# Both group norms of a hybrid attention/LRU layer: root and reciprocal on all partitions, in place of a column that is spread afterwards

## The chip, the cores and the metric

The kernel runs on one core of one Trainium2 chip. The metric is the device time of one execution in microseconds (us). The engines are named as in the profile: PE is TensorE (PEld its weight loads), ACT is ScalarE, DVE is VectorE, POOL is GpSimd, and SP is the engine whose queue issues most of the DMAs.

## The reference

One layer of an encoder: a norm, one input projection, attention on one half of the channels, a gated linear recurrence (LRU) on the other half, a norm of each half, a gate, and the output projection. Sequence 512, model width 2048, all in float32.

```python
def rms_norm(x, w):
    xf = x.astype(jnp.float32)
    y = xf * lax.rsqrt(jnp.mean(xf * xf, axis=-1, keepdims=True) + EPS)
    return (y * w.astype(jnp.float32)).astype(x.dtype)

def hybrid_layer(x, norm_w, w_in, ...):
    h = rms_norm(x, norm_w)
    proj = jnp.einsum('bsd,de->bse', h, w_in)
    q, k, v, g_attn, xr, g_lru = jnp.split(proj, SPLITS, axis=-1)
    attn_out = attention_group(q, k, v, q_norm_w, k_norm_w)      # 1024 channels
    lru_out = lru_group(xr, conv_w, conv_b, ...)                  # 1024 channels
    mixed = jnp.concatenate([rms_norm(attn_out, attn_norm_w) * jax.nn.silu(g_attn),
                             rms_norm(lru_out, lru_norm_w) * jax.nn.silu(g_lru)], axis=-1)
    return x + jnp.einsum('bse,ed->bsd', mixed, w_out)
```

The change concerns the two `rms_norm` calls on `attn_out` and `lru_out`: for each of the 512 tokens, one number, 1/sqrt(mean of 1024 squares + EPS).

## The kernel before

**Layout.** Both groups' outputs lie with channels on the 128 partitions and tokens along the free axis (128x512 tiles), so the sum of squares of one token runs over partitions as well as over tiles. Tiles are first squared and added (on ACT, DVE and POOL) into one 128x512 tile: `sums["l"]` (named `hsum` in the trace) for the LRU group, `sums["a"]` (`asum`) for the attention group. What is left is a sum over the 128 partitions for each of 512 tokens, the root and the reciprocal, and the result laid on all partitions as `gbc` (128x512), since every channel of a token is multiplied by it (`normed`).

**How the norm is made.** `group_rstd` multiplies four 128x128 blocks of the sums, as stationary operands, by a column of ones (`L817`), which puts tokens on partitions: a 128x4 tile `r_l` or `r_a`. DVE copies it from PSUM, POOL does the mean and the power -0.5 (`rsqrt_mean`, L343 and L344). `rows` then splits the four columns into a high and a low part, writes each into a diagonal (`ident` times the column, L357), and multiplies a matrix of ones by both (L364), so that the 512 numbers stand on all partitions; DVE copies that into `gbc` (L365).

**The float32 scheme.** Each product of two float32 matrices is three products of their high and low parts (`mm3`, L153 to L155). Of each weight tile `wr` that a DMA brings, ACT writes the high part `wh` (L218) and DVE the low part `wl` (L219); PE reads both. Work on PE is thus a steady stream of 128x512 products, each of which needs such a pair.

**What sets the order.** PE's instructions stand in the order in which the program writes them (generators `weave` fill work into a chain by counted steps, the numbers that `yield` returns). On ACT, DVE and POOL a scheduler chooses the order when the kernel is built; what stands in `tc.high_priority` goes ahead. On the chip each engine runs its instructions strictly in that order, and one that waits holds up all behind it.

**PSUM.** There are eight banks: four of kind `pj` for the projections and four of kind `mm`. A projection keeps four `pj` banks for its four token blocks or column blocks; the next projection writes the same four, so each must have been read out ("evacuated") before. For the query projections ACT does that (`ev<-pj`, L593); for the gate projections DVE does (L468).

**Where the two norms stand.** The LRU group's norm is in `kv`: `lru_squares` ends with an addition on POOL (L567), and the norm is made while the second query projection runs (its banks are those of the first query projection). The attention group's norm is in `later`, beside the last gate projection; its sum ends with an addition on POOL (L750) after the last attention head.

Of the kernel before, what the change touches and what calls it, by code (L numbers as in the profile page):

```python
# [12 lines left out]
F32R = mybir.dt.float32r  # L13
AF = mybir.ActivationFunctionType
# [3 lines left out]
P = 128  # L18
SEQ = 512
DM = 2048  # L20
KT = DM // P
NT = SEQ // P
HD = 128
NH = 8
NKV = 2
G = NH // NKV
NB = 8
EPS = 1e-6
# [35 lines left out]
def hybrid_kernel(  # L64
# [20 lines left out]
    nc = tc.nc  # L85
# [4 lines left out]
    pools, order = {}, {"left": [], "right": []}  # L90

    def opened(name, side):
        pools[name] = tc.alloc_tile_pool(name=name, bufs=1, side=side, reuse_waits="tile")
        order[side].append(name)
        return pools[name]
# [22 lines left out]
    def nm(s):  # L118
        cnt[0] += 1
        return f"{s}_{cnt[0]}"  # L120
# [22 lines left out]
    def mm():  # L143
        return ps.tile([P, SEQ], F32, tag="mm", name=nm("mm"))

    def const(shape, name, dt=F32):
        return cp.tile(list(shape), dt, tag=name, name=name)

    def f(ap):
        return ap.bitcast(F32)  # L150
# [9 lines left out]
    ones = const([P, P], "ones")  # L160
    nc.gpsimd.memset(ones, 1.0)
    ones_r = const([P, P], "ones_r", F32R)
# [178 lines left out]
    def rsqrt_mean(dst, src, n, width):  # L341

        nc.gpsimd.tensor_scalar(dst, src, 1.0 / n, EPS, op0=ALU.mult, op1=ALU.add)  # L343
        last_pool[0] = nc.gpsimd.tensor_tensor(dst, dst, nhalf[:, :width], op=ALU.pow).ins  # L344
# [4 lines left out]
    def rows(dst, col, dg):  # L349

        shape = [P, NT, P]
        part = [const([P, NT], nm("part")) for _ in range(2)]
        parts = [dg() for _ in part]
        nc.vector.tensor_copy(part[0].bitcast(F32R), col)
        nc.vector.tensor_sub(part[1], col, part[0])
        for c, d in zip(part, parts):
            nc.vector.tensor_mul(  # L357
                d, ident[:, None, :].broadcast_to(shape), c[:, :, None].broadcast_to(shape)
            )
        yield  # L360
        pb = mm()
        for k, d in enumerate(parts):
            d = d.rearrange("p t q -> p (t q)")
            nc.tensor.matmul(pb, ones_r, d, start=k == 0, stop=k == 1)  # L364
        nc.vector.tensor_copy(dst, pb)  # L365
        yield
# [59 lines left out]
    def drain(fill):  # L426
        for _ in fill:
            pass
# [30 lines left out]
    sums = {}  # L459
# [97 lines left out]
    def lru_squares():  # L557

        hsum = pools["rot"].tile([P, 2, SEQ], F32, tag="hsum", name="hsum")
        nc.scalar.activation(hsum, hp[0], AF.Square)  # L560
        for pair in hp[1:]:
            yield 2
            sq = pools["rot"].tile([P, 2, SEQ], F32, tag="hsq", bufs=1, name=nm("hsq"))
            nc.scalar.activation(sq, pair, AF.Square)
            nc.vector.tensor_add(hsum, hsum, sq)
        sums["l"] = hsum[:, 0, :]
        nc.gpsimd.tensor_add(sums["l"], sums["l"], hsum[:, 1, :])  # L567
# [29 lines left out]
    def norm_rope(es, nh, tab):  # L597

        es = [e[:, : nh * HD].rearrange("p (h d) -> p h d", d=HD) for e in es]
        rs = []  # L600
        for e in es:
            r = pools["rot"].tile([P, nh], F32, tag=f"rr{nh}", bufs=NT, name=nm("rr"))
            for h in range(nh):
                sq = pools["rot"].tile([P, HD], F32, tag="sh", bufs=1, name=nm("sh"))
                nc.scalar.activation(sq, e[:, h, :], AF.Square, accum_out=r[:, h : h + 1])
            rsqrt_mean(r, r, HD, nh)
            rs.append(r)
        for t, (e, r) in enumerate(zip(es, rs)):
            sq = pools["rot"].tile([P, nh, HD], F32, tag="sq", bufs=2, name=nm("sq"))
            nc.vector.tensor_mul(e, e, r[:, :, None].broadcast_to([P, nh, HD]))  # L610
            for s in range(2):
                nc.vector.tensor_mul(
                    sq.rearrange("p h (a s d) -> p h a s d", s=2, d=32)[:, :, :, s, :],
                    e.rearrange("p h (a s d) -> p h a s d", s=2, d=32)[:, :, :, 1 - s, :],
                    tab[:, t, 1, :].rearrange("p (a s d) -> p a s d", s=2, d=32)[:, None, :, s, :]
                    .broadcast_to([P, nh, 2, 32]),
                )
            nc.vector.tensor_mul(e, e, tab[:, t, 0, :][:, None, :].broadcast_to([P, nh, HD]))
            nc.vector.tensor_add(e, e, sq)
        return es  # L620
# [7 lines left out]
    def sent(es, nh, *us):  # L628

        us = us or [  # L630
            pools["rot"].tile([P, NQ, 2, NT, B], F32, tag="uq", bufs=2, name=nm("uq"))
            for _ in range(nh // 2)
        ]
        for n, u in enumerate(us):
            for t, e in enumerate(es):
                blocks(u, t, e[:, 2 * n : 2 * n + 2].rearrange("p h d -> p (h d)"))
            yield
            asides.append(put_aside(u, "qd", 5))

    def landed(aside_):  # L640

        to = pools["qkv"].tile([P, NQ, 2, NT, B], F32, tag="lq", bufs=2, name=nm("lq"))
        bring_back(to, aside_)
        return to

    def split_head(pair, k, hi, lo):
        src = pair[:, :, k]
        hi, lo = (in_order(v) for v in (hi, lo))
        nc.scalar.copy(hi, src)
        nc.vector.tensor_sub(lo, src, f(hi))  # L650

    def kv(es):
        turned_k = sent(norm_rope(es, NKV, rk), NKV)
        yield 20
        opened("wx", "right")
        for t in range(NT):
            vv = es[t][:, NKV * HD :]
            vt = aside(
                lambda *a: pools["qkv"].tile(*a, tag="v", bufs=NT, name=nm("v")), 2 * NKV * HD // H
            )  # L660
            vh[t], vl[t] = vt[:, 0, :], vt[:, 1, :]
            nc.scalar.copy(vh[t], vv)
            nc.vector.tensor_sub(vl[t], vv, f(vh[t]))
        yield from lru_squares()
        yield 2
        drain(turned_k)
        yield 6
        pair = landed(asides.pop(0))
        for h in range(NKV):
            yield (12, 4)[h]  # L670
            kt = pools["qkv"].tile([P, 2, SEQ], F32R, tag="kt", bufs=NKV, name=nm("kt"))
            kth[h], ktl[h] = kt[:, 0, :], kt[:, 1, :]
            split_head(pair, h, kth[h], ktl[h])
        r = group_rstd(sums["l"], "r_l", NB * P)
        yield 4
        drain(rows(
            gbc, r,
            lambda: pools["rope"].tile([P, NT, P], F32R, tag="kv", bufs=NT, name=nm("kv")),
        ))

    qs = {}

# [127 lines left out]
    def fin_s(shape=(P, SEQ), dt=F32):  # L810
        return pools["fin"].tile(list(shape), dt, tag="s", bufs=2, name=nm("s"))

    def group_rstd(src, name, n):

        pr = mm()
        for t in range(NT):
            nc.tensor.matmul(  # L817
                pr[:, t : t + 1], src[:, t * P : (t + 1) * P], ones[:, 0:1], start=True, stop=True
            )
        r = const([P, NT], name)  # L820
        nc.vector.tensor_copy(r, pr[:, :NT])
        rsqrt_mean(r, r, n, NT)
        return r

    gbc = const([P, SEQ], "gbc")

    def normed(pair):
        nc.vector.tensor_mul(pair, pair, gbc[:, None, :].broadcast_to([P, 2, SEQ]))
# [22 lines left out]
    def aside(tile_of, n):  # L851

        t = tile_of([P, n * H + 16], F32R)
        return t[:, 8 : 8 + n * H].rearrange("p (n e) -> p n e", e=H)
# [403 lines left out]

    fill = with_sums(both(), 3)
    weave(fill, kv(kvs))  # L1260
    drain(fill)

# [67 lines left out]
    def build(i, pair, parts):  # L1330
        mixed[i][1] = parts
        seven(pair, *parts)
# [4 lines left out]


    def later():
        yield 2  # L1340
        with tc.high_priority():
            r = group_rstd(sums["a"], "r_a", NH * HD)
        yield 4
        with tc.high_priority():
            drain(rows(gbc, r, lambda: fin_s((P, NT, P), F32R)))
        for pair in ap_[:2]:
            normed(pair)
        yield 4
        todo = gate(late, ap_[:2], R_AN, fin_s)
        for _ in range(3):  # L1350
            yield next(todo)
        build(4, ap_[0], [hring.tile([P, 7, H], F32R, name=nm(t)) for t in ("mh", "ml")])
        yield from todo
        for pair in ap_[2:]:
            normed(pair)

    acc = []
    wsums = last_sums()
    fill = with_sums(proj_feat(C_GA + SEQ, acc, take=take), 1, 8, 8 + 2 * NP)
    weave(fill, later())  # L1360
    drain(fill)
    closed("xw")
# [71 lines left out]
```

## Time and profile before

| | |
|---|---|
| median of 3 runs | 632.08 us (631.41 to 632.18) |
| the profiled execution | 632.23 us, of which the span is 630.1 us |
| PE | 623.8 us busy, 99% of the span, 2771 instructions |
| DVE | 491.4 us, 78%, 796 instructions |
| ACT | 348.2 us, 55%, 612 instructions |
| POOL | 104.4 us, 17%, 137 instructions |

Times in the profile are counted from the start of the span. A row of the timeline reads: start, duration, engine, line, operation, output<-input, shapes, count of merged instructions, and in square brackets the idle time of the engine before it with what ended it. Instructions on one engine overlap by some 0.08 us, so what an instruction adds on a busy engine is the distance between starts, not its duration.

### The profile page before, as it was taken

The numbers are of one execution on the slowest core, as the hardware profiler recorded it, in microseconds if no ns is written. First come the engines' busy times: TensorE is split into PE (matmuls) and PEld (weight loads), VectorE is DVE, ScalarE is ACT, GpSimd is POOL, SyncE is SP. The second block draws the span as 40 slices with busy tenths as digits, with TensorE's granted clock in tenths as the row PEclk, the third lists the DMA queues.
The fourth block names the chain that finished last, engine by engine and source line by source line (L and its number), as shares of the span: only waits on it lengthen the run. The fifth ranks groups of instructions, "written<-read, shape, count | busy, mean of one in ns | idle before, by whom it ended". The sixth has DMA issues, their size and how long they took to land.

```text
span 630.1 us, 8302 instructions
## 1 busy us (share of the span) xinstructions
PE 623.8 (99%) x2771; PEld 514.1 (82%) x2771; DVE 491.4 (78%) x796; ACT 348.2 (55%) x612; POOL 104.4 (17%) x137
## 2 busy tenths in 40 slices
PE   9999999999999999999999999999999999999997
PEld 6888888888888888888888888888888888888885
DVE  5967979986699874887887888549978866886885
ACT  3764899479945812545475447435445534443441
POOL 0000210112003632622123222100300001010010
PEclk9999999999999999999999999999999999999999
DMA  8977786859774599479668646924995677896162
GB/s 288 305 206 227 182 195 166 184 134 193 238 232 136 169 247 236 97 206 273 183 177 252 201 141 191 262 76 127 236 242 185 212 249 243 285 323 235 68 200 100
DMA packets 73594, 127.61 MB, mean 203 GB/s; under 512 B 6616, under 2 KB 29264, under 8 KB 73552
## 3 DMA queue, kind: packets, MB, share of 16 engines
q1 hardware_dynamic: 65664, 109.65, 55.8%
q0 software_dynamic: 7712, 17.31, 14.2%
q8 instruction: 21, 0.34, 0.2%
q14 instruction: 21, 0.17, 0.1%
q10 hardware_dynamic: 176, 0.14, 0.1%
HBM read 110.29 MB, written 37.75 MB: 235 GB/s over the span
## 4 chain that ended last, share of the span: by engine, by line
PE 96%; DMA 2%; SPq 1%; DVE 1%; issue 0%; DVEq 0%
PE pj L153 20%; PE pj L155 20%; PE pj L154 20%; PE mm L1023 14%; PE pj L1023 10%; PE mm L155 3%; PE mm L153 3%; PE mm L154 3%; DMA b<-in_x_dram 2%; SPq L206 0%; SPq L240 0%; PE mm L817 0%; DVE xu L281 0%; PE mm L364 0%; DVE b L272 0%
## 5 line engine op out<-in xcount | busy, mean ns | idle before, releaser
L154 PE MATMUL pj<-x,wh 128*128 128x512 f32 x376 | 146.6, 390 | 0.3 <-DVE x L261 0.3
L153 PE MATMUL pj<-x,wh 128*128 128x512 f32 x376 | 146.9, 391 | 0.0
L155 PE MATMUL pj<-x,wl 128*128 128x512 f32 x376 | 146.5, 390 | 0.2 <-DVE wl L219 0.2
L218 ACT CAST wh<-wr 128x512 fp32r<-128x512 f32 x143 | 85.7, 617 | 95.0 <-PE pj L154 37.0
L219 DVE TENSOR_TENSOR wl<-wr,wh 128x512 fp32r<-128x512 f32 x144 | 100.1, 723 | 20.0 <-ACT wh L218 19.2
L875 ACT CAST wh<-wr 128x1024 fp32r<-128x1024 f32 (+1 forms) x72 | 60.7, 860 | 75.0 <-PE mm L1023 37.5
L876 DVE TENSOR_TENSOR wl<-wr,wh 128x1024 fp32r<-128x1024 f32 (+1 forms) x72 | 68.7, 985 | 29.6 <-ACT wh L875 29.5
L155 PEld LDWEIGHTS pj<-x,wl 128*128 128x128 f32 x376 | 70.6, 188 | 15.4 <-DVE wl L219 0.6
L154 PEld LDWEIGHTS pj<-x,wh 128*128 128x128 f32 x376 | 70.6, 188 | 15.2 <-DVE x L261 0.7
L153 PEld LDWEIGHTS pj<-x,wh 128*128 128x128 f32 x376 | 70.6, 188 | 14.9
L153 PE MATMUL pj<-wh,x 128*128 128x512 f32 x192 | 74.8, 390 | 0.0
L155 PE MATMUL pj<-wh,x 128*128 128x512 f32 x192 | 74.7, 389 | 0.0
L154 PE MATMUL pj<-wl,x 128*128 128x512 f32 x192 | 74.7, 389 | 0.0
L899 POOL DMA_DIRECT2D t<-in_w_out_dram x40 | 33.7, 916 | 142.8 <-DMA t<-in_w_out_dram 99.3
L1023 PE MATMUL mm<-wh,ml 128*128 128x512 f32 x128 | 49.8, 389 | 0.0
L1023 PE MATMUL mm<-wh,mh 128*128 128x512 f32 x128 | 49.8, 389 | 0.0
L1023 PE MATMUL mm<-wl,mh 128*128 128x512 f32 x128 | 49.8, 389 | 0.0
L155 PEld LDWEIGHTS pj<-wh,x 128*128 128x128 f32 x192 | 36.0, 188 | 7.5
L153 PEld LDWEIGHTS pj<-wh,x 128*128 128x128 f32 x192 | 36.1, 188 | 7.5
L154 PEld LDWEIGHTS pj<-wl,x 128*128 128x128 f32 x192 | 36.1, 188 | 7.4
L705 POOL TENSOR_SCALAR p<-p,sm 128x512 f32<-128x512 f32 x32 | 24.2, 761 | 90.1 <-DVE sm L704 90.1
L1023 PE MATMUL pj<-wh,mh 128*128 128x512 f32 x96 | 37.4, 389 | 0.0
(209 smaller groups left out, 1035.2 us busy)
## 6 DMA issues: line engine op xcount, KB each, us to landing
wr<-in_w_in_dram SPq DMA_DIRECT2D x71, 512.0 KB, 5.0
wr<-in_w_out_dram SPq DMA_DIRECT2D x24, 512.0 KB, 5.3
t<-in_w_out_dram POOLq DMA_DIRECT2D x40, 256.0 KB, 7.5
wr<-t SPq DMA_DIRECT2D x40, 256.0 KB, 5.6
pd<-u SPq DMA_DIRECT2D x16, 512.0 KB, 3.0
pt<-pd SPq DMA_DIRECT2D x64, 128.0 KB, 4.0
t<-in_w_out_dram SPq DMA_DIRECT2D x24, 256.0 KB, 5.5
t<-t SPq DMA_DIRECT2D x16, 256.0 KB, 5.4
```

The costliest lines, as they stand in the source:

```text
L153: nc.tensor.matmul(acc, lh, rh, start=start, stop=False)
L154: nc.tensor.matmul(acc, lh, rl, start=False, stop=False)
L155: nc.tensor.matmul(acc, ll, rh, start=False, stop=stop)
L218: copy(hi, raw[:, k, :]).ins,
L219: nc.vector.tensor_sub(lo, raw[:, k, :], f(hi)).ins,
L705: last_pool[0] = nc.gpsimd.tensor_scalar(p, p, sm, 0.0, op0=ALU.mult, op1=ALU.add).ins
L875: nc.scalar.copy(hi[:, to], b)
L876: nc.vector.tensor_sub(lo[:, to], b, f(hi[:, to]))
L899: nc.gpsimd.dma_start(dst, src, accum_op=ALU.add)
L1023: nc.tensor.matmul(dst[s], lh[:, ts_], rh, start=i == 0 and j == 0, stop=i == 7 and j == 2)
```

## The change

`group_rstd` is gone, and the two norms don't use `rows` any more (it remains for the first norm, `rbc`). In their place stand `halved` and `spread`. `halved` splits the 128x512 sum into a high part (a copy on ACT) and a low part (a subtraction on DVE). `spread` multiplies the matrix of ones by both parts (two products, 128x512), which sums over the partitions and leaves each token's sum on all of them; ACT takes the root of sum/n + EPS from PSUM into `gbc` (it needs `eps`, a new 128x1 tile that POOL sets at the start), and DVE takes the reciprocal of `gbc` in place, 128x512. Nothing of it is left to POOL.

In `kv` the products stay where those of `rows` stood; in `later` they move six steps ahead, to where the four small products stood, and `halved` ahead of that.

```diff
@@ kv
-        r = group_rstd(sums["l"], "r_l", NB * P)
+        parts = halved(
+            sums["l"],
+            lambda: pools["rope"].tile([P, SEQ], F32R, tag="kv", bufs=NT, name=nm("kv")),
+        )
         yield 4
-        drain(rows(
-            gbc, r,
-            lambda: pools["rope"].tile([P, NT, P], F32R, tag="kv", bufs=NT, name=nm("kv")),
-        ))
+        spread(gbc, parts, NB * P)
@@
-    def group_rstd(src, name, n):
-
-        pr = mm()
-        for t in range(NT):
-            nc.tensor.matmul(
-                pr[:, t : t + 1], src[:, t * P : (t + 1) * P], ones[:, 0:1], start=True, stop=True
-            )
-        r = const([P, NT], name)
-        nc.vector.tensor_copy(r, pr[:, :NT])
-        rsqrt_mean(r, r, n, NT)
-        return r
+    eps = const([P, 1], "eps")
+    nc.gpsimd.memset(eps, EPS)
+
+    def halved(src, tile_of):
+
+        hi, lo = tile_of(), tile_of()
+        nc.scalar.copy(hi, src)
+        nc.vector.tensor_sub(lo, src, f(hi))
+        return hi, lo
+
+    def spread(dst, parts, n):
+
+        pb = mm()
+        for k, part in enumerate(parts):
+            nc.tensor.matmul(pb, ones_r, part, start=k == 0, stop=k == 1)
+        nc.scalar.activation(dst, pb, AF.Sqrt, scale=1.0 / n, bias=eps)
+        nc.vector.reciprocal(dst, dst)
@@ later
+        with tc.high_priority():
+            parts = halved(sums["a"], lambda: fin_s(dt=F32R))
         yield 2
         with tc.high_priority():
-            r = group_rstd(sums["a"], "r_a", NH * HD)
+            spread(gbc, parts, NH * HD)
         yield 4
-        with tc.high_priority():
-            drain(rows(gbc, r, lambda: fin_s((P, NT, P), F32R)))
         for pair in ap_[:2]:
             normed(pair)
```

Three places of the built programs show what that does to the order.

The first is ACT where the first query projection ends (from 204 us in the trace before). `hsq` are squares for the LRU sum, `wh` high parts of weights, `ev<-pj` the evacuations of the first query projection's banks. Before:

```order
L564 ACTIVATE hsq_2040<-hs_1699 128x1024
L218 CAST wh_2273<-wr_2271 128x512
L218 CAST wh_2277<-wr_2271 128x512
L593 ACTIVATE ev_2101<-pj_1765,rstd 128x512
L605 ACTIVATE sh_2110,rr_2109<-ev_2101 128x128
```

and now:

```order
L564 ACTIVATE hsq_2042<-hs_1701 128x1024
L218 CAST wh_2275<-wr_2273 128x512
L819 CAST kv_2372<-hsum 128x512
L218 CAST wh_2279<-wr_2273 128x512
L593 ACTIVATE ev_2103<-pj_1767,rstd 128x512
L605 ACTIVATE sh_2112,rr_2111<-ev_2103 128x128
```

The high part of the LRU sum (`kv<-hsum`), which reads what POOL's last addition writes, now stands ahead of one `wh` and of the first evacuation.

The second is DVE beside the last gate projection (from 424 us). `ev<-pj` evacuates a bank, `t` and `ml` belong to the output's operands made from `hs` (their line numbers are six higher now), and `wl_4216` and `wl_4220` are now the names of what were `wl_4226` and `wl_4230`: the low parts of the weights of the gate projection's third pair of rows. Before:

```order
L846 TENSOR_TENSOR t_911_4270<-hs_1086,t_911_4270 128x256
L354 CAST part_4393<-r_a 128x4
L849 TENSOR_TENSOR ml_4269<-hs_1086,mh_4268 128x768
L355 TENSOR_TENSOR part_4394<-r_a,part_4393 128x4
L357 TENSOR_TENSOR s_4395<-ident,part_4393 128x512
L357 TENSOR_TENSOR s_4396<-ident,part_4394 128x512
L219 TENSOR_TENSOR wl_4226<-wr_4223,wh_4225 128x512
L219 TENSOR_TENSOR wl_4230<-wr_4223,wh_4229 128x512
L849 TENSOR_TENSOR ml_4259<-t_908_4260,mh_4258 128x1024
L849 TENSOR_TENSOR ml_4269<-t_911_4270,mh_4268 128x1024
L365 COPY gbc<-mm_4401 128x512
```

and now, from `ev_4312` on:

```order
L468 TENSOR_TENSOR ev_4312<-pj_3814,rbc 128x512
L219 TENSOR_TENSOR wl_4169<-wr_4162,wh_4168 128x512
L855 TENSOR_TENSOR ml_4249<-hs_889,mh_4248 128x768
L855 TENSOR_TENSOR ml_4249<-t_905_4250,mh_4248 128x1024
L850 TENSOR_TENSOR t_908_4260<-hs_1088 128x512
L855 TENSOR_TENSOR ml_4259<-hs_1088,mh_4258 128x768
L851 TENSOR_TENSOR t_908_4260<-hs_1088,t_908_4260 128x256
L850 TENSOR_TENSOR t_911_4270<-hs_1448 128x512
L852 TENSOR_TENSOR t_908_4260<-hs_1088,t_908_4260 128x256
L851 TENSOR_TENSOR t_911_4270<-hs_1448,t_911_4270 128x256
L855 TENSOR_TENSOR ml_4269<-hs_1448,mh_4268 128x768
L829 RECIPROCAL gbc<-gbc 128x512
```

Behind these stand `wl_4216` and `wl_4220`. The low parts, which stood behind the two diagonals, now stand behind the reciprocal and behind more of the work on `hs`. Ahead of these rows, between `ev_4306` and `ev_4312`, stand now the low part `s_4315<-asum` (new), one `t` (128x512) with its two 128x256 steps, two evacuations and one `wl`.

The third is ACT at the same place. Before, one table load stood ahead of two SiLUs (`s<-ev`); now:

```order
L854 CAST mh_4248<-t_905_4250 128x1024
L804 ACT_TABLE_LOAD
L804 ACTIVATE s_4421<-ev_4306 128x512
L828 ACT_TABLE_LOAD
L828 ACTIVATE gbc<-mm_4344,eps 128x512
L218 CAST wh_4215<-wr_4213 128x512
L218 CAST wh_4219<-wr_4213 128x512
L854 CAST mh_4258<-t_908_4260 128x1024
L804 ACT_TABLE_LOAD
L804 ACTIVATE s_4462<-ev_4308 128x512
```

The root stands between the two SiLUs, with a table load ahead of each of the three; at the LRU group's place the root has none.

## The prediction, as put on record

> **What bounds the kernel now.** I read the page first (busy shares, granted clock, the chain that ended last), then PE's waits (us in total, times, longest), then the chain in order of time (start, us), then the timelines at the two places. The first three lines are of the page, the next three the waits, the last the chain:
>
> ```profile
> PE 623.8 (99%) x2771; PEld 514.1 (82%) x2771; DVE 491.4 (78%) x796; ACT 348.2 (55%) x612; POOL 104.4 (17%) x137
> PEclk9999999999999999999999999999999999999999
> PE 96%; DMA 2%; SPq 1%; DVE 1%; issue 0%; DVEq 0%
> ...
> PE mm L1141 <- POOL ones L161: 1.1, 1, 1.1
> PE pj L154 <- DVE x L261: 0.3, 1, 0.3
> PE pj L155 <- DVE wl L219: 0.2, 1, 0.2
> ...
> 473.12 2.72 PE mm L1023 x12
> ```
>
> PE is the bound, at full clock in every slice, and its three waits come to 1.6 us, all of it early. A product takes 2.72/12 = 0.2267 us. So the time changes by what PE no longer has to do, and by any wait that PE gets: nothing downstream has slack in which a wait of PE could vanish. Other engines count only where they make PE wait.
>
> **Removed from PE.** The four small products stand as one row, x8, at each place (timeline of PE):
>
> ```profile
> 232.37 0.95 PE L817 MATMUL mm<-ones,hsum 128*128 128x1 f32 x8
> 233.18 0.47 PE L153 MATMUL pj<-wh,x 128*128 128x512 f32 x1
> 233.49 0.39 PE L154 MATMUL pj<-wl,x 128*128 128x512 f32 x1
> ...
> 430.74 0.95 PE L817 MATMUL mm<-ones,asum 128*128 128x1 f32 x8
> 431.55 0.48 PE L153 MATMUL pj<-x,wh 128*128 128x512 f32 x1
> 431.87 0.39 PE L154 MATMUL pj<-x,wh 128*128 128x512 f32 x1
> ```
>
> From the start of the small products to the second product behind them it is 1.12 and 1.13 us, of which one ordinary product is 0.23: 0.89 + 0.90 = 1.8 us go. The two products with the matrix of ones remain at each place, with other inputs and the same shapes. Sum so far: 632.23 - 1.8 = 630.4.
>
> **Place one: the high part of the LRU sum on ACT.** It reads what POOL's last addition (L567) writes, and stands ahead of a `wh` and of the evacuations of the first query projection. Behind the waiting copy is thus everything for which PE waits before it may write those four banks again. The timelines of DVE, POOL, ACT and PE there:
>
> ```profile
> 206.32 2.39 DVE L219 TENSOR_TENSOR wl<-wr,wh 128x512 fp32r<-128x512 f32 x2
> 206.54 1.62 POOL L567 TENSOR_TENSOR hsum<-hsum 128x512 f32<-128x512 f32 x1 [8.25 <-issue]
> 205.02 1.12 ACT L218 CAST wh<-wr 128x512 fp32r<-128x512 f32 x2
> 206.05 0.68 ACT L593 ACTIVATE ev<-pj,rstd 128x512 f32<-128x512 f32 x1
> 210.18 0.69 ACT L593 ACTIVATE ev<-pj,rstd 128x512 f32<-128x512 f32 x1
> 223.72 1.30 ACT L218 CAST wh<-wr 128x512 fp32r<-128x512 f32 x2 [3.36 <-PE pj L155]
> 207.88 0.39 PE L153 MATMUL pj<-wh,x 128*128 128x512 f32 x1
> ```
>
> When does PE need the first bank? In PE's order the first product into it stands 108 rows ahead of the small products: 232.37 - 108 x 0.2267 = 207.89, which is the row at 207.88. Before, the first evacuation ends at 206.73, 1.15 us early. Now ACT has its first `wh` done by 205.6 and then waits for POOL, which ends at 206.54 + 1.62 = 208.16 (nothing ahead of it changes, so that stays). Two copies back to back out of idleness take 1.30 (the row at 223.72), the evacuation begins 0.09 before the second ends (as at 206.05 against 206.14) and takes 0.68: 208.2 + 1.30 - 0.09 + 0.68 = 210.1. PE waits 210.1 - 207.9 = 2.2 us. The other banks follow in step: the fourth evacuation starts 4.13 behind the first and its bank is due 18 products, 4.08 us, behind the first, which adds 0.05. With the handover I take 2.3 us; bounds 2.0 (POOL's row rough by 0.3) and 2.6 (a weight load that waits too). The rest of ACT's delay (some 3.3 us on `wh`, squares and the query's norms) dies out: ACT stands idle 3.36 us ahead of the row at 223.72, and the `wh` that it makes next are due some 10 us later, two pairs of weight rows of 24 products (5.4 us) each. If that cover were gone, the price would be PE's wait for a `wh`; the idle row says it isn't.
>
> The rest at place one costs nothing on PE. The root (no table load) stands between two `wh`, where ACT idles; the reciprocal replaces a copy, and the low parts behind it belong to a projection that starts some 60 products after the products with ones. POOL loses two small instructions and issues its DMAs earlier; SP's copies `t<-t` trade places with one `wr`, which goes earlier.
>
> **Place two: the reciprocal on DVE.** The new products now stand where the small ones stood (430.74). Their inputs are ready: POOL's last sum ends at 424.4, the copy on ACT follows, and the low part stands on DVE two rows behind the `ev` at 424.90. What matters is `wl_4216` behind the reciprocal. Reciprocals there are only small ones. Two lines of the source view (ns min/median/max), the copy of the same shape by form, and the timelines of DVE, POOL and ACT:
>
> ```profile
> L704 DVE RECIPROCAL sm<-sm x32: 119/156/167, 272.0 to 394.6; 128x1 f32<-128x1 f32 x32
> L443 DVE RECIPROCAL lc<-lc x1: 253/253/253, 63.1 to 63.1; 128x16 f32<-128x16 f32 x1
> ...
> L365 DVE COPY gbc<-mm 128x512 f32<-128x512 f32 x2 | 1.4, 687 | 2.3 <-PE mm L364 2.3
> ...
> 424.90 0.68 DVE L468 TENSOR_TENSOR ev<-pj,rbc 128x512 f32<-128x512 f32 x1
> 425.50 0.68 DVE L844 TENSOR_TENSOR t<-hs 128x512 f32<-128x512 f32 x1
> 426.10 0.95 DVE L849 TENSOR_TENSOR ml<-hs,mh 128x768 fp32r<-128x768 f32 x1
> 426.97 1.28 DVE L468 TENSOR_TENSOR ev<-pj,rbc 128x512 f32<-128x512 f32 x2
> 428.17 0.41 DVE L845 TENSOR_TENSOR t<-hs,t 128x256 f32<-128x256 f32 x1
> 428.50 0.68 DVE L844 TENSOR_TENSOR t<-hs 128x512 f32<-128x512 f32 x1
> ...
> 436.86 2.35 DVE L849 TENSOR_TENSOR ml<-t,mh 128x1024 fp32r<-128x1024 f32 x2
> 439.13 0.68 DVE L365 COPY gbc<-mm 128x512 f32<-128x512 f32 x1
> ...
> 423.14 1.29 POOL L750 TENSOR_TENSOR asum<-asum,p 128x512 f32<-128x512 f32 x1 [15.41 <-ACT p L749]
> 431.36 2.00 ACT L848 CAST mh<-t 128x1024 fp32r<-128x1024 f32 x2 [2.75 <-DVE t L846]
> 435.07 1.28 ACT L804 ACT_TABLE_LOAD   x1
> ```
>
> From one element to 16 a reciprocal grows by 253 - 156 = 97 ns, 6.5 ns an element: 156 + 511 x 6.5 = 3.5 us for 128x512. The lower end of the 128x1 row (119) gives 8.9 ns and 4.7 us, the upper (167) 5.7 and 3.1; were it like the copy of that shape, 0.69. I take 3.5, since two rows of the operation itself stand behind it; the copy is the far low end.
>
> [...]
>
> When does it start? Starts on DVE are 0.60 apart for 128x512 (424.90, 425.50, 426.10), 0.87 for 128x768, 0.33 for 128x256, 1.14 for 128x1024 (436.86 to 439.13 for two). Between the `ev` at 424.90, itself counted, and the reciprocal stand ten of the first, three of the second, five of the third, one of the fourth: 6.0 + 2.6 + 1.7 + 1.1 = 11.4, so it starts at 436.3, some 436.4 with a small wait. The root is ready before: PE's products end by 431.4, SiLU, a table load (1.28) and the root bring it to 434. So `wl_4216` ends at 436.4 + 3.5 - 0.08 + 0.69 = 440.5. Its product stands 40 rows behind the first product with ones: 430.74 + 40 x 0.2267 = 439.8. PE waits 0.7 us; 0.3 to 1.9 with the bounds 3.1 and 4.7, and 0 if the reciprocal takes under 2.8. `wl_4220` ends 0.6 later and is due 0.7 later, so one wait covers both. The next pairs are due 5.4 us (24 products) apart, and DVE needs some 5 for what stands between them, so nothing more waits; the operands made from `av` are due only after 473. Three table loads for one (2.6 us more) lie in ACT's idle time there (2.75 ahead of the row at 431.36); gone that cover, PE would wait for a `wh`. DVE's copy, diagonals and small steps go; the count is of the new order, so that is in it already.
>
> **The sum.** 632.23 - 1.8 + 2.3 + 0.7 = 633.4 for the profiled execution, which stands 0.15 above the median of the runs. Against that median of 632.08: **633.3 us**, 1.2 us or 0.19% slower. A measurement of this kernel can tell about 0.2% (1.26 us) from no change, so the likeliest case lies on that line; its own range is 632.8 to 634.0.
>
> **Rivals.**
>
> *Only the first wait.* If DVE reaches the reciprocal 0.7 us earlier than counted, or it takes under 2.8 us, PE waits at place one alone: 632.08 - 1.8 + 2.3 = 632.6, within 0.2%. For it: my start adds 19 steps. Against: the two rows of reciprocals. Chance 0.24.
>
> *A slower reciprocal.* 8 to 9 ns an element (the lower 128x1 row) make 4.4 to 4.7 us, and the wait at place two 1.6 to 1.9: 634.2 to 634.5. It decides from 8 ns on. Chance 0.14. [...]
>
> *PE is slow for a while behind the wait at place one.* At the start of the span, out of idleness, PE's products take longer than the same ones a little later, whatever the granted clock says (timeline of PE):
>
> ```profile
> 3.81 1.09 PE L253 MATMUL mm<-ident,b 128*128 128x128 f32 x4
> 7.13 0.60 PE L253 MATMUL mm<-ident,b 128*128 128x128 f32 x4
> ```
>
> Four take 1.09 and then 0.60, so PE worked at 0.55 of its speed for up to 7 us. If 2.3 us of idleness bring that back for as long as the wait lasted, or for three times that, 0.45 of it is lost: 1.0 to 3.1 us, so 634.3 to 636.4. The longest wait of PE before is 1.1 us, at the very start, so no row shows what 2.3 do. [...] Chance 0.05.
>
> *Neither wait: faster.* If the copy of the sum didn't hold the evacuations, only the 1.8 us would count: 630.3. It would need POOL to end before 206, and POOL starts at 206.54; or PE to have another bank free, and the order reuses the four. Chance 0.07.
>
> The forecast keeps 0.50, over the line in half of it: slower 0.25 + 0.14 + 0.05, and 0.06 more for waits of PE that I didn't see, taken from no change: 0.50; same 0.25 + 0.24 - 0.06 = 0.43; faster 0.07. The range 632.2 to 634.6 leaves out the faster rival and most of the slow PE.
>
> **What would show it.** No L817; PE's waits with ACT `ev` L593 at about 2.3 us, four times at most, near 207.9; ACT's `kv<-hsum` waiting for POOL some 2.6 us; a reciprocal of about 3.5 us, twice; PE L155 waiting for DVE `wl` L219 for 0.7 us near 441 (each step of place two 1.4 us later than in the text, since PE comes later). Wrong: no wait at 207.9, or waits of PE that name DMAs, the root, or the output's operands.

## The result, and the profile after

The changed kernel takes 638.23 us (median of 4 runs, 638.18 to 638.38) against 632.06 us (631.41 to 632.18) for the kernel before: ratio 1.0100, 95% interval 1.0088 to 1.0112. It is slower, as forecast, but by 6.2 us and not by 1.2, and lies outside the range of 632.2 to 634.6. The profiled execution has a span of 636.5 us; before it was 630.1.

The page after (busy time and the granted clock in 40 slices), and below it all of PE's waits (us in total, times, longest):

```profile
PE 629.0 (99%) x2755; PEld 512.3 (80%) x2755; DVE 493.4 (78%) x788; ACT 353.5 (56%) x618; POOL 101.9 (16%) x134
PEclk9999999999999999999999999999999999999999
...
PE pj L153 <- ACT ev L593: 1.2, 1, 1.2
PE mm L1147 <- POOL ones L161: 1.1, 1, 1.1
PE pj L155 <- DVE wl L219: 0.5, 2, 0.3
```

PE is busy in every slice at the full granted clock (9 in each slice, 0.998 over the span; before 1.000). It runs 16 records fewer, it waits 2.8 us in all where it waited 1.6, and still it needs 5.2 us more of busy time. The waits have grown by 1.2 us, less than the 1.8 us of small products that went: the products themselves have become longer.

The two places that the prediction spoke of look as it said. Place one, timelines of POOL, ACT and PE:

```profile
206.55 1.62 POOL L567 TENSOR_TENSOR hsum<-hsum 128x512 f32<-128x512 f32 x1 [8.26 <-PE pj L155]
...
208.20 0.62 ACT L819 CAST kv<-hsum 128x512 fp32r<-128x512 f32 x1 [2.57 <-POOL hsum L567]
208.73 0.61 ACT L218 CAST wh<-wr 128x512 fp32r<-128x512 f32 x1
209.25 0.68 ACT L593 ACTIVATE ev<-pj,rstd 128x512 f32<-128x512 f32 x1
...
208.42 0.40 PE L155 MATMUL pj<-wh,x 128*128 128x512 f32 x1
209.98 0.51 PE L153 MATMUL pj<-wh,x 128*128 128x512 f32 x1 [1.16 <-ACT ev L593]
```

The copy on ACT waits 2.57 us for POOL's last addition, the evacuation behind it begins at 209.25 (206.05 before), and the product into its bank at 209.98; 210.1 was worked out, and before it was 207.88. But of these 2.1 us PE waits only 1.16: its last product ahead of it begins at 208.42, so it comes to this place 0.8 us later than before. Place two, the source view of the reciprocal (ns min/median/max), DVE's and PE's timelines:

```profile
L829 DVE RECIPROCAL gbc<-gbc x2: 3347/3350/3353, 242.2 to 440.0; 128x512 f32<-128x512 f32 x2
...
428.60 0.68 DVE L468 TENSOR_TENSOR ev<-pj,rbc 128x512 f32<-128x512 f32 x1
440.04 3.35 DVE L829 RECIPROCAL gbc<-gbc 128x512 f32<-128x512 f32 x1
443.30 2.43 DVE L219 TENSOR_TENSOR wl<-wr,wh 128x512 fp32r<-128x512 f32 x4
...
443.99 0.50 PE L155 MATMUL pj<-x,wl 128*128 128x512 f32 x1 [0.33 <-DVE wl L219]
```

The reciprocal takes 3.35 us, starts 11.44 us behind the evacuation from which it was counted (11.4), and PE waits 0.33 us for the weight behind it.

Where the time is lost shows in a stretch in which the change moves nothing. PE's instructions in 140 us of the output projection and in 40 us of the first projections, which lie ahead of everything that the change touches except the setting of `eps` at 1.6 us; before, then after (columns: stretch, PE busy and instructions, clock, DMA share, GB/s):

```profile
480.00:620.00 140.00, 140.00 (x619) 1.00 0.65 214
60.00:100.00 40.00, 40.00 (x179) 1.00 0.79 200
...
480.00:620.00 140.00, 140.00 (x607) 1.00 0.66 217
60.00:100.00 40.00, 40.00 (x177) 1.00 0.79 199
```

Twelve products fewer in 140 us, with no wait, the same clock and nearly the same DMA traffic: 140/619 = 226.2 ns for one before, 140/607 = 230.6 after. Neither waits nor instructions differ there. What does differ is where the tiles lie in SBUF. The change takes the two columns `r_l` and `r_a` and four `part` tiles out of the pool of constants and puts `eps` in, each taking 32 bytes of a partition. Everything allocated on the left behind that pool (most raw weights, most split weights `wh` and `wl`, the `x2` tiles, the tiles of the query's rotation and of the LRU's sum, part of the output's operands) moves down by 160 bytes, while the pools on the right (some of the split weights, the LRU's and the attention's tiles, the rest of the output's operands) stay. That became the theory 'addresses'; the rival was that the changed instructions make PE slow.

### The profile page after: what moved, and what is told of

The parts are those of the page before. It is cut to its first block, busy times and chain, and to the rows that moved or that the text cites. A ratio compares the mean times of both kernels' runs of the same rounds, so it can differ in the third digit from the quotient of the medians.

```text
span 636.5 us, 8266 instructions
## 1 busy us (share of the span) xinstructions
PE 629.0 (99%) x2755; PEld 512.3 (80%) x2755; DVE 493.4 (78%) x788; ACT 353.5 (56%) x618; POOL 101.9 (16%) x134
## 4 chain that ended last, share of the span: by engine, by line
PE 95%; DMA 1%; DVE 1%; SPq 1%; issue 0%; ACT 0%; POOL 0%; DVEq 0%
PE pj L155 20%; PE pj L153 20%; PE pj L154 20%; PE mm L1029 14%; PE pj L1029 10%; PE mm L154 4%; PE mm L155 4%; PE mm L153 3%; DMA b<-in_x_dram 1%; SPq L206 1%; DVE gbc L829 0%; SPq L240 0%; POOL hsum L567 0%; DVE xu L281 0%; DVE b L272 0%
## 5 line engine op out<-in xcount | busy, mean ns | idle before, releaser
L219 DVE TENSOR_TENSOR wl<-wr,wh 128x512 fp32r<-128x512 f32 x144 | 98.5, 714 | 22.4 <-ACT wh L218 21.3
L1029 PE MATMUL pj<-wh,ml 128*128 128x512 f32 x96 | 37.9, 395 | 0.0
```

The lines of the kernel that those rows point to most:

```text
L219: nc.vector.tensor_sub(lo, raw[:, k, :], f(hi)).ins,
L1029: nc.tensor.matmul(dst[s], lh[:, ts_], rh, start=i == 0 and j == 0, stop=i == 7 and j == 2)
```

## The experiments

**The changed kernel, tiles moved back.** Behind the constant `asum`:

```diff
     sums["a"] = const([P, SEQ], "asum")
+    const([P, 40], "lpad")
```

Expected: 

> The changed kernel with 160 bytes of unused constants behind the others, so that the raw weights, the split weights, x2 and all that stands on the left above them lie at the addresses of the kernel before. Theory 'addresses' (the change cost 632.7 - 632.06 = 0.6 us by its own instructions: -1.8 for the eight small products, +2.1 for the evacuation wait, +0.3 for the reciprocal; the rest, 5.6 us, comes from products that run 1 to 7 ns longer because moving and stationary tile lie at different places within 64 bytes): 632.4 to 633.2 us, and consecutive 128x512 products 226.6 to 227 ns apart between 60 and 100 us, where the changed kernel has 229. Rival 'instructions' (the new work itself, by its waits, lets TensorE run slower): 638 us as the changed kernel, since every instruction is the same.

Measured: 632.20 us (10 runs, 631.63 to 634.33), ratio to the kernel before 1.0009 (0.9998 to 1.0020), 0.2 us below what was expected. Not one instruction differs from the changed kernel, and 6.0 us are gone. Stretches as above, and PE's first wait:

```profile
480.00:620.00 140.00, 140.00 (x619) 1.00 0.66 214
60.00:100.00 40.00, 40.00 (x178) 1.00 0.78 199
...
PE pj L153 <- ACT ev L593: 1.5, 1, 1.5
```

The 619 products are back. The rival falls.

**The kernel before, tiles moved by 32 bytes.** The same line with `const([P, 8], "lpad")`.

Expected: 

> The kernel before with 32 bytes of unused constants: the same left-hand tiles move by 32 bytes, no instruction changes. Theory 'addresses': the same pairs of tiles differ within 64 bytes as in the changed kernel (644 of 2693 wide products whose moving tile and the next product's stationary tile differ by 32, 97 in the kernel before), so 632.06 + 5.6 = 637.7 us (637.0 to 638.4). Rival 'instructions': 632.1 us, no change.

Measured: 637.96 us, ratio 1.0098 (1.0082 to 1.0113). In 480 to 620 us:

```profile
480.00:620.00 140.00, 140.00 (x608) 1.00 0.65 214
```

So 32 unused bytes cost the kernel before what the change cost it.

**The changed kernel, right-hand tiles moved too.**

```diff
-    opened("pad", "right").tile([P, 8], F32, name="pad")
+    opened("pad", "right").tile([P, 16], F32, name="pad")
```

Expected: 

> The changed kernel with the right-hand pools moved by 32 bytes too, so that nearly all operands of TensorE lie at 32 modulo 64, moving and stationary alike (103 pairs of 2693 differ, against 644). Theory 'addresses' in the form 'moving against stationary': what counts is that the two agree, so 632.4 to 633.4 us as with the tiles moved back. In the form 'each tile wants a multiple of 64': all products are now slow, 638 us or more (2693 x 6.9 ns = 18 us at most: 650). Rival 'instructions': 638 us.

Measured: 635.78 us, ratio 1.0060 (1.0045 to 1.0075), between the forms. Its stretches:

```profile
480.00:620.00 140.00, 140.00 (x609) 1.00 0.65 214
60.00:100.00 40.00, 40.00 (x178) 1.00 0.79 200
```

From 60 to 100 us it has the 178 products of the kernel with its tiles moved back, although all operands lie at 32 modulo 64; so places off a multiple of 64 are no harm in themselves. In the output projection, where left and right tiles are mixed, it is slow although both lie at 32 modulo 64. The left has moved down by 160 bytes and the right by 32, so there they differ by 128: agreement within 64 bytes isn't enough.

**The kernel before, x2 moved by 32 bytes against the weights.** An unused tile `[P, 8]` ahead of the first `x2` in its pool; `x2` and the rotation's and the LRU sum's tiles above it on the left move, the weights stay.

Expected: 

> The kernel before with 32 bytes of unused space between the split weights and the x2 tiles: only x2 (and what stands on the left above it, for the LRU and q/k stages) moves by 32 bytes; weights stay at multiples of 64. Now 1817 pairs of 2693 differ by 32 within 64 bytes against 97. Form 'moving against stationary' at 6.9 ns a pair: 632.06 + 1720 x 0.0069 = 643.9 us (642 to 646). Form 'each tile wants a multiple of 64': fewer tiles are off than with 32 bytes of constants, so at most 638. Rival 'instructions': 632.1.

Measured: 642.75 us, ratio 1.0171 (1.0156 to 1.0187).

```profile
480.00:620.00 140.00, 140.00 (x619) 1.00 0.68 224
60.00:100.00 40.00, 40.00 (x174) 1.00 0.81 197
```

Five products fewer in the first projections, where `x2` meets the weights, and none in the output projection, which has no `x2`. Fewer tiles moved than with 32 bytes of constants, and it costs nearly twice as much: what counts is the two operands against each other.

**The products by themselves.** A kernel of nothing but 128x512 products, 64 for each pair of places:

```python
for m, s in ROWS:                      # places of the moving and of the stationary tile, in bytes
    for i in range(EACH):              # 64 products, four tiles of each in turn
        product(i, m[i % 2], s[i % 2])
```

Expected: 

> No part of the layer is computed: 128x512 products only, 64 for each row of a table of places (moving tile and stationary tile, in bytes behind a multiple of 2048), each product with a new stationary tile. Theory 'moving against stationary, within 64 bytes': 226.7 ns a product where the two differ by 0 or a multiple of 64, 233 ns where they differ by 4, 16, 32, 96 or 160. Theory 'within 256 bytes' (the moved-right run left products 231 to 232.5 ns apart where the two differed by 128): 226.7 only at 0, 256, 512 and 1024. Theory 'each tile by itself': 32 and 32, 128 and 128 slow as well. With alternating places (even products 0, odd ones 128): if a product's moving tile meets the stationary tile that is loaded beside it, for the next product, then moving (0,128) with stationary (128,0) is the fast one; if it meets its own, moving (0,128) with stationary (0,128).

Measured in one execution, from the starts of the first and the last product of each 64 (ns a product):

```
moving minus stationary, bytes   0      4      16     32     64     96     128    160    192
ns                               226.7  237.0  231.5  233.3  229.1  233.3  233.2  234.3  233.4
                                 256    384    512    1024   stationary moved: 32 128  both: 32     128
ns                               227.0  233.3  226.9  226.7                 233.3 232.4     227.4  227.4
even/odd places: moving 0,128 with stationary 0,128: 228.5; with 128,0: 230.1; with 0,0: 230.0;
moving 0,0 with stationary 0,128: 232.1;  first row again, at the end: 226.7
```

Two stretches of the timeline, 61 products merged into one row each (512 bytes apart, then 128):

```profile
182.70 13.99 PE L98 MATMUL bank<-ops 128*128 128x512 f32 x61
108.38 14.39 PE L98 MATMUL bank<-ops 128*128 128x512 f32 x61
```

With a multiple of 256 bytes between the two a product took 226.7 to 227.0 ns, at every other distance that was tried 229.1 to 237.0, 2 to 10 ns more, and with both moved alike 227.4, 0.7 ns more than with both at 0. In twelve stretches of 13 us between 31 and 280 us the granted clock is 1.00, no engine but PE is busy (0.00 us) and the DMA share is at most 0.01, so it is PE against itself. The alternating rows don't tell which product's stationary tile a moving tile meets: all four lie between the ends.

**The kernel before, moved by 64 and by 256 bytes.**

Expected for 64: 

> The kernel before with 64 bytes of unused constants instead of 32. Theory 'within 64 bytes': the pairs agree as in the kernel before, so 631.9 us. Theory 'within 256 bytes': left and right tiles differ by 64, so the same 550 pairs more are slow as with 32 bytes, 636 to 638 us.

Expected for 256: 

> The kernel before with 256 bytes of unused constants. Theory 'within 64 bytes' and theory 'within 256 bytes': 631.9 us, no change. Theory 'any distance from the old place' (512 or more, or the addresses as such): 636 to 638 us.

Measured: 635.91 us, ratio 1.0063 (1.0048 to 1.0079), and 631.84 us, ratio 0.9999 (0.9990 to 1.0008). In the output projection, 64 bytes first:

```profile
480.00:620.00 140.00, 140.00 (x612) 1.00 0.65 214
480.00:620.00 140.00, 140.00 (x620) 1.00 0.65 214
```

So in the kernel too 256 bytes cost nothing (620 products, where before had 619), and 64 bytes cost 4.0 us (612 products). (64 bytes came out just below the expected 636 to 638 us: the products by themselves lost least at that distance, 2.4 ns.)

With the starts of all products from the traces and the addresses of the built programs, the theory can be held against every run. A pair is counted as differing where a product's moving tile and the next product's stationary tile, or those of the pair ahead of it, aren't a multiple of 256 bytes apart; the sum is over some 2665 wide products that follow each other without a wait, time above 226.67 ns:

```
kernel                       differ   ns each   agree ns   above 226.67, us   time against before, us
before                        113      232.7     226.9       1.3                0
changed                       787      233.2     228.2       8.0               +6.2
changed, moved back           113      232.6     227.0       1.4               +0.4
before, moved by 32           783      232.8     228.2       7.6               +6.1
before, moved by 64           785      230.5     228.1       5.7               +4.0
changed, right moved by 32    787      232.3     227.3       5.6               +3.9
before, x2 moved by 32       1851      233.2     227.2      12.5              +10.9
before, moved by 256          113      232.7     227.0       1.4               -0.1
```

For the kernels without the change, the column above 226.67 ns, less the 1.3 of before, gives the last column within 0.4 us. The changed ones come out 0.8 to 0.9 us shorter than with their own +0.4 on top; 0.3 to 0.4 of that is PE's wait at place one, which shrinks from 1.5 to 1.2 and 1.1 us where PE comes there late; the other 0.5 stays open.

Products that agree are slower too in the mixed kernels (228.2): those that follow a differing one. They make some 2 of the 6.7 us that the changed kernel has more in that column. The timeline of PE shows it, in the changed kernel and then before:

```profile
63.10 0.40 PE L155 MATMUL pj<-x,wl 128*128 128x512 f32 x1
63.34 0.39 PE L153 MATMUL mm<-k,k 128*128 128x512 f32 x1
65.42 0.39 PE L153 MATMUL mm<-k,k 128*128 128x512 f32 x1
...
63.49 0.39 PE L155 MATMUL pj<-x,wl 128*128 128x512 f32 x1
63.72 0.39 PE L153 MATMUL mm<-k,k 128*128 128x512 f32 x1
65.76 0.39 PE L153 MATMUL mm<-k,k 128*128 128x512 f32 x1
```

The product at 63.10 has both tiles on the left, at 32 modulo 256, and the next one, at 63.34, has both on the right, at 192. Each agrees within itself; only the moving tile of the one and the stationary tile of the other differ, by 96 bytes. So neighbours count, and not a product's own two tiles alone. The ten products from 63.10 to 65.42 take 2.32 us, and before, where all these tiles lie at 192, the same ten take 2.27. Eight such changes of side between 60 and 100 us make the 0.4 us, two products, that the stretch lost. Where the two sides are 128 bytes apart (right moved by 32 too), only two products behind such a change are slow, 233 and 231 ns, which is why that kernel's first projections look undisturbed.

**The first wait taken away.** The rounded copy of the LRU sum is put behind the four evacuations on ACT's queue, with the tiles moved back:

```diff
-                nc.scalar.activation(e, acc[t], AF.Identity, scale=rstd[:, t : t + 1])
+                last_ev[:] = [nc.scalar.activation(e, acc[t], AF.Identity, scale=rstd[:, t : t + 1]).ins]
...
-        parts = halved(
+        with behind(last_ev):
+            parts = halved(
```

Expected: 

> The changed kernel with its tiles moved back and the LRU sum's rounded copy put on ScalarE's queue behind the four evacuations that it held up. Theory 'addresses plus one wait': the 1.5 us of TensorE's wait for ev near 208 us go, 632.2 - 1.5 = 630.7 us (630.4 to 631.2), a little faster than the kernel before (631.84). Rival: the evacuations are late for another reason, or the copy's new place delays the half that is subtracted on VectorE and with it weights: 632 us or more.

Measured: 630.15 us, ratio 0.9974 (0.9964 to 0.9984): faster than the kernel before, and 0.25 us below what was expected. ACT's timeline, the first evacuation and the copy:

```profile
206.00 0.68 ACT L593 ACTIVATE ev<-pj,rstd 128x512 f32<-128x512 f32 x1
211.53 0.61 ACT L820 CAST kv<-hsum 128x512 fp32r<-128x512 f32 x1
```

The evacuation begins at 206.0 again and PE's wait for `ev` is gone. That is 2.05 us less than with the tiles moved back, 0.5 more than the wait of 1.5. The timeline of the changed kernel with tiles moved back says where it goes:

```profile
206.87 0.39 PE L155 MATMUL pj<-wh,x 128*128 128x512 f32 x1
208.77 0.50 PE L153 MATMUL pj<-wh,x 128*128 128x512 f32 x1 [1.51 <-ACT ev L593]
209.10 0.39 PE L154 MATMUL pj<-wl,x 128*128 128x512 f32 x1
215.42 0.39 PE L154 MATMUL pj<-wl,x 128*128 128x512 f32 x1
```

A row of PE is 0.39 us long, but without a wait the next starts 0.2267 behind it. The wait in brackets counts from the end of the row, so by the starts PE loses more: 208.77 - 206.87 - 0.23 = 1.67 us. From 208.77 to 209.10 it loses another 0.1, and the 27 products from 209.10 to 215.42 take 0.234 us each, 0.2 more, although their tiles agree. Together that is 2.0 of the 2.05 us.

**The attention group's norm alone**, in the kernel before, weights and `x2` at the old addresses.

Expected: 

> The kernel before with the attention group's norm changed and the LRU group's norm as it was, weights and x2 at their old addresses. By the prediction's terms: half of the small products go, -0.9 us, and the reciprocal of 3.35 us delays one pair of weights by 0.3 us (0.7 as predicted): 631.9 - 0.6 = 631.3 us (631.0 to 631.7). Rival 'the reciprocal costs as much as the products gave': 631.9.

Measured: 631.12 us, ratio 0.9989 (0.9980 to 0.9998). PE's wait at the reciprocal:

```profile
439.11 0.39 PE L154 MATMUL pj<-x,wh 128*128 128x512 f32 x1
439.80 0.50 PE L155 MATMUL pj<-x,wl 128*128 128x512 f32 x1 [0.30 <-DVE wl L219]
```

0.8 us gained of 0.9; the interval (0.1 to 1.3 us) holds the 0.6 that was worked out. By the starts the wait costs 439.80 - 439.11 - 0.23 = 0.46 us, and 0.6 with the slow products behind it, which would leave 0.3 us of gain; the interval holds that too.

**The best version.** The kernel with the first wait taken away, and `v` without its 32 bytes of space in front:

```diff
-        t = tile_of([P, n * H + 16], F32R)
-        return t[:, 8 : 8 + n * H].rearrange("p (n e) -> p n e", e=H)
+        return tile_of([P, n * H], F32R).rearrange("p (n e) -> p n e", e=H)
```

(and an unused tile of 64 floats ahead of `v`, so that nothing else moves).

Expected: 

> The last kernel (630.15 us: tiles moved back, LRU copy behind the evacuations), and the four tiles v laid on multiples of 256 bytes from the others instead of 32, 96, 160 and 224 bytes off. Theory 'within 256 bytes': the last 113 wide products whose places differ, 232.6 ns each in that run, come down to 226.9, and the few products behind them too: 0.65 to 0.9 us less, 629.3 to 629.5 us. Rival: v was laid aside for ScalarE's and VectorE's writes, and these lose more than TensorE wins: 630.2 us or more.

Measured: 629.10 us, ratio 0.9955 (0.9943 to 0.9968): 2.8 us less than the kernel before, 9.1 less than the changed one, and 0.2 below what was expected. Only 9 differing products are left, and the sum above 226.67 ns falls from 1.3 to 0.4 us: 0.9 of the 1.05 us gained.

## Why the prediction was right or wrong

**The step that failed** is the first: "the time changes by what PE no longer has to do, and by any wait that PE gets". It took 0.2267 us a product from the trace of before as a constant of the chip, at full clock. The runs show that figure only where a product's moving tile and the next one's stationary tile lie a multiple of 256 bytes apart (226.7 to 227.0 ns in the products by themselves, 229 to 237 elsewhere), as nearly all did before. By freeing 192 bytes of constants and adding 32 the change moved the left-hand tiles alone, and 674 products more, with those behind them, cost 6.7 us in the trace. No rival had it; the 0.06 for "waits of PE that I didn't see" was for waits, and there is none. The diff showed the removed tiles, and the kernel's pools stand in a row, so it could have been read that the left moves and the right doesn't; that this costs time no row of before said openly, though its products with `v`, which lies off the others, were 233 ns apart there. That the kernel came out clearly slower, in the direction of the forecast, is chance: what the sum has in it came to 0.4 us, hardly to be told from nothing, and the other 6 us are a term that it doesn't have.

Whether it is the load of the next stationary tile that the running product meets, and in what part of the memory, the runs don't show: they show only the two operands' distance and the time.

**The removed products**, 1.8 us: right within the interval. The kernel without the first wait is 1.75 us faster than before, with the second wait, some 0.6 us by the starts, still in it; the interval of its ratio allows 1.0 to 2.3, so 1.6 to 2.9 for the products.

**Place one**, 2.3 us (2.0 to 2.6): right in mechanism, at the lower bound in size. In the changed kernel POOL's end, the copy's wait and the evacuation's start came within 0.2 us of what was worked out. With the tiles moved back the wait cost 1.67 us by the starts and 2.0 with the slow products behind it, and taking it away gave 2.05. That 1.67 and not 2.2 us went into the wait itself is in part luck of the execution: POOL ended 0.28 us after PE's need in the trace of before and 0.14 us ahead of it in this one, where the evacuation came 0.2 us sooner too. In the changed kernel the wait shows as 1.2 and not as 1.5 because PE is late there already, so less of ACT's delay is left to wait for: the longer products hid 0.35 us of it.

**Place two**, 0.7 us: right in mechanism, and nearly in size. The count of DVE's steps was exact (11.44 against 11.4), the reciprocal took 3.35 us and not 3.5, and PE's wait of 0.3 us cost 0.5 by the starts, 0.6 with the slow products behind it. The slope from the two small rows held: (3350 - 156)/511 = 6.25 ns an element against 6.5. The rival of a slower reciprocal, which decides from 8 ns on, falls. (Its 8 to 9 ns make 4.2 to 4.8 us, and not 4.4 to 4.7 as its sum has it; of that sum only the upper end, 8.9 ns and 4.7 us, stands on a row, the 119 ns for one element. No run shows its 4.4 us; the runs showed 3.35.)

**The other rivals.** 'PE slow behind the wait' is there, at some 0.3 us where 1.0 to 3.1 were worked out: it is no large term. 'Only the first wait' is nearly what the changed kernel is with its tiles moved back: 632.2 us against 632.6. 'Neither wait' was worked out as 630.3, and the kernel that has only the small second wait took 630.15.

So the change's own instructions cost 0.4 us (-0.1 to 1.3 by the interval), which by this measurement is hardly to be told from nothing; the 6 us of the verdict are the layout.

## What to carry to other kernels

A change that adds or drops even a 32-byte constant moves every tile allocated behind it; in this kernel, which TensorE bounds, 32 unused bytes cost 6.1 us (637.96 against 631.84). Where TensorE bounds a kernel, compare the addresses of its operands before and after, and pad the constants so that moving and stationary tiles stay a multiple of 256 bytes apart, as in the products above that took 226.7 to 227.0 ns and not 229 to 237. A verdict on an edit is a verdict on its layout too, until the same edit has been timed with the old addresses. And look for products whose spacing differs at the same clock: here 113 of them in the kernel before, all but 9 of them with `v`, were worth 1 us. All of this was measured on 128x512 products of float32 parts, each with a new stationary tile; other shapes and types weren't tried.

## What the runs showed of the hardware that was not expected

- TensorE's 128x512 products with a new stationary tile each took 226.7 to 227.0 ns with the two operands 0, 256, 512 or 1024 bytes apart within a partition, and 229 to 237 ns at 4, 16, 32, 64, 96, 128, 160, 192 and 384; with both at 32 or both at 128 they took 227.4. The granted clock was 1.00 in the twelve stretches above, so it doesn't show this.
- One pair of neighbours at 96 bytes from each other made a run of ten products slow, 2.32 us where it was 2.27; at 128 bytes only two products were slow, 233 and 231 ns.
- Behind a wait of 1.5 us PE's products took 0.234 us each for some 6 us, at agreeing places and a granted clock of 1.00 (190 to 250 us).
- The distance of the tiles is not seen as a wait and hardly in the duration of a product's row (0.39 or 0.40 us), only in how many products fit into a stretch (607 in 140 us where 619 were).
- A 128x512 reciprocal on VectorE took 3.35 us, nearly five times the copy of that shape (0.69).
